# A planner's queue rule: of the operations that wait for a busy engine, the one that is due first goes first; attention is prepared five units ahead

## The chip, the cores and the metric

One core of a Trainium2 chip runs the kernel. The metric is the device time of one execution in microseconds (us), as the median of several. The engines that matter are PE (matrix products), DVE, ACT and POOL (elementwise work), and SP, which issues most DMAs. Each works through its own list of instructions in order; semaphores make an instruction wait for another engine.

## The reference

A decoder layer over 512 tokens of width 1024. After an RMS norm one projection gives the inputs of two attention mixers, eight heads of 64 each: one over blocks (here with its top-k taking every past block), one with three branches (compressed, selected, window). Gates and two more projections follow.

```python
h = rms_norm(x, norm_w[l]); proj = h @ w_in[l]
(q_a, k_a, v_a, z_a, q_b, kc, vc, ksl, vsl, kwn, vwn, gate_b, z_b, gate_m) = jnp.split(proj, split_points, axis=-1)
o_a = moba_mixer(rms_norm(heads(q_a), q_norm_a[l]), rms_norm(heads(k_a), k_norm_a[l]), heads(v_a), bias_a)
k_cmp = rms_norm(compress(heads(kc), cmp_pos_k[l], cmp_w1_k[l], cmp_w2_k[l]), k_norm_cmp[l])
v_cmp = compress(heads(vc), cmp_pos_v[l], cmp_w1_v[l], cmp_w2_v[l])
o_b = nsa_mixer(...)
y_a = o_a * jax.nn.silu(z_a); y_b = o_b * jax.nn.silu(z_b)
g_m = jax.nn.sigmoid(gate_m)
merged = g_m[..., :D_MODEL] * (y_a @ w_branch_a[l]) + g_m[..., D_MODEL:] * (y_b @ w_branch_b[l])
x = x + merged @ w_out[l]
```

All of it is float32. The kernel gets that accuracy from pairs of rounded numbers: a value is split into a high part (a rounded copy) and a low part (the value less that copy), and a product is three matmuls: high by high, low by high, high by low.

## The kernel before, in words

**Work.** Weights come from memory as 128x512 tiles (`wr`, six buffers). Each is split: a copy makes the high part `wh` (L350 on ACT or L354 on POOL), a subtraction the low part `wl` (L359, on DVE or POOL). The same two steps make `vh` and `vl` for the hidden layer of the compression (matmuls L839, L840). PE then runs the products (L384). Gate and output projections use a seven-product scheme for 2x2 block matrices, whose sums of weights are made in memory by DMAs that POOL and ACT issue (L572, L573).

**Attention** is 24 units: eight heads of the first mixer (units 0 to 7), then two groups of four heads with two branches each (units 8 to 15 and 16 to 23). A unit is, for four blocks of queries, scores (`sps`, L1001, L1002), bias and maximum (`sb`, L1020, DVE), exponential (`P`, L1035, ACT), reciprocal (L1038, DVE), scaling (L1039, POOL), and then transposes (`pt`, L1048), their split (`ph` L1060 on ACT, `pl` L1062 on DVE) and the products with the values (`O`, L1082). Before a unit can begin, its keys and queries are prepared: PE transposes them (`pq`, L924), ACT copies the high parts (`ks`, L955), DVE subtracts (`kx`, L957), ACT copies those to the other half of the partitions (`kx`, L960). The first unit of a group also needs the compressed scores (`scp`, L1180) and a softmax over them (`sc`, L1185 to L1204).

**Order.** Nothing is scheduled on the chip. While the program is written, a planner in it keeps a clock, `now`, and for ACT, DVE and POOL the time at which each comes free, from costs written in the code. PE's list is merged from several streams (attention, projections, compression): a stream whose next matmul has been ready for `MARGIN` ns is taken, by shares. All work of the other engines comes in chains (class `Chain`): steps that follow one another. A heap holds the chains by the time at which their next step can begin. `Chain.step` picks, of the engines that a step may run on, the one that would end it first, and books that engine at once, even if it is busy for some time yet. So steps are served in the order in which they became ready. Two kinds of chain are the exception: the splits of weights (`SLACK`, 3 us in all) and the prepared sums of the input (`XSLACK`, 4 us) step back while their engine is busy.

```python
end, k = min((ends(k, c.t, n), k) for k, n in cost.items())
wait = free[k.upper()] - 40 - c.t
if wait > 0 and c.slack > 0:
    c.slack -= wait
    c.t += wait
    c.push()
    return
```

The costs that the planner gives a 512-wide subtraction are 65 + 1.045 x 512 = 600 ns on DVE and 180 + 2.08 x 512 = 1245 ns on POOL (`either`). A rounded copy of a weight tile costs it 520 ns on ACT and 590 ns on POOL (L349 ff.).

While unit n runs, attention also drives the preparation of later units (`poll`, in `attention`): of the units n+1 up to n+`UNITS`-1 the first whose preparation is unfinished gets a step.

Of the kernel before, what the change touches and what calls it, by code (L numbers as in the profile page):

```python
# [38 lines left out]
SLACK = 3e3  # L39
XSLACK = 4e3  # L40
# [16 lines left out]
UNITS = 4  # L57
# [10 lines left out]
MARGIN = 600  # L68
# [36 lines left out]
def hybrid_kernel(ctx: ExitStack, tc: tile.TileContext, x, x0, xT, wtok, wchan, wz, wgate, gains, w1,  # L105
# [63 lines left out]
    class Chain:  # L169


        def __init__(c, t=None, held=False, slack=0.0):
            c.slack = slack
            c.t = now[0] if t is None else t
            c.q = deque()
            c.held = held
# [6 lines left out]
        def push(c):  # L183
            heapq.heappush(heap, (c.t, next(seq), c))
# [27 lines left out]
        def step(c):  # L212
# [10 lines left out]
            if cost is None:  # L223
                fn()
            else:
                if now[0] > 30e3:
                    cost = {k: n * SLOW[k.upper()] for k, n in cost.items()}
                end, k = min((ends(k, c.t, n), k) for k, n in cost.items())
                wait = free[k.upper()] - 40 - c.t
                if wait > 0 and c.slack > 0:  # L230
                    c.slack -= wait
                    c.t += wait
                    c.push()
                    return
                if k in lock:
                    lock[k] = end
                free[k.upper()] = end
                c.t = end + OUT[k.upper()] + LAT
                fn(ENG[k])
# [21 lines left out]
    def run_until(t):  # L261
        now[0] = max(now[0], t)
        while heap and heap[0][0] <= now[0]:
            heapq.heappop(heap)[2].step()
# [51 lines left out]
    class Stream:  # L316
# [19 lines left out]
        def split(w, upto):  # L336
            while len(w.chain) < min(upto, len(w.raws)):
# [8 lines left out]
                c = w.chain[i] = Chain(max(now[0], t), slack=SLACK if w is not W1_[0] and now[0] > 30e3 else 0.0)  # L346
# [367 lines left out]
    def proj_norm(name, gi, tags="gggg"):  # L714
        toks[name] = [None] * NT

        def emit(t, ps):
            toks[name][t] = att(name, F32)
            ch = Chain(now[0] + 230)
# [14 lines left out]
    def proj_v(name, outs, first=False):  # L734
# [3 lines left out]
        def emit(t, ps):  # L738
            ch = Chain(now[0] + 230)
# [56 lines left out]
    def compress_w(kv):  # L796
# [3 lines left out]
        def emit(ps):  # L800
            ch = Chain(now[0] + 230)
            for g in range(2):
                for l in range(2):
# [6 lines left out]
                    ch.do({"D": 335}, f, ps if g and l else None, None if g or l else "gmt")  # L810
            for i8 in range(2):
# [284 lines left out]
    def o_out(O, m, h):  # L1096
# [5 lines left out]
        ch = Chain(now[0] + 230)  # L1102
# [14 lines left out]
    def y_try(k):  # L1117
        if ("ys",) + k in done and ("zs",) + k in done:
            y, z = ys[k], zs[k]
            ch = Chain(max(done[("ys",) + k], done[("zs",) + k]))  # L1120
# [3 lines left out]
    def y_split(k):  # L1124

        def f():
            y, hi, lo = ys[k], att("yh"), att("yl")
            ch = Chain(max(now[0], done[("ym",) + k]))
# [221 lines left out]
    def x_prep(k):  # L1350
# [14 lines left out]
        c = Chain(held=True, slack=XSLACK)  # L1365
# [234 lines left out]
    def m_sums(k, fs):  # L1600
# [6 lines left out]
        c, d = x_sums(x1, x2, ta, tb)  # L1607
        for n_ in range(2):
            hi_lo(c, ta[:, h[n_]], ts[0][1][:, h[n_]], ts[0][2][:, h[n_]], n_)
# [193 lines left out]
```

## Time and profile before

| what | us |
|---|---|
| median of 3 runs (456.24 to 456.89) | 456.74 |
| the profiled execution's own time | 456.11 |
| its span, first to last instruction | 454.3 |
| first matmul with data begins | 4.50 |
| last matmul begins | 450.56 |
| PE clock granted | 1.00 throughout |

Times in the views are counted from the start of the span. The profiled execution has 1.8 us around its span and lies 0.63 us under the median. A matmul's end is modelled in the profile and matmuls overlap, so the distance from one matmul's start to the next tells more than its busy time: in an undisturbed stretch a 128x512 product begins every 0.23 us and a 128x256 product every 0.12 us, though they are shown as 0.40 and 0.28 us long.

### The profile page before, as it was taken

Reading aid. Unit: us, or ns where it says so; the run is one execution under the profiler, and the core shown is the slowest. Engines: PE = TensorE matmul, PEld = TensorE weight load, DVE = VectorE, ACT = ScalarE, POOL = GpSimd, SP = SyncE. Lnnn points to the kernel's source line nnn. Section 1 sums busy time; section 2 is a strip of 40 time slices with the busy share of each in tenths; the row PEclk is TensorE's granted clock in tenths of the full one; section 3 lists DMA queues with packets and bytes.
Section 4 is the critical chain, followed back from the end, with each engine's and each line's share of the span. In section 5 each row is a group of like instructions: output and inputs, shape, how many; then the busy total and the mean of one; then the engine's idle time right before and its main releaser. Section 6 shows DMA issues by size and latency. Waiting matters only on the chain.

```text
span 454.3 us, 8535 instructions
## 1 busy us (share of the span) xinstructions
PE 446.8 (98%) x2779; PEld 397.5 (87%) x2779; DVE 383.5 (84%) x938; ACT 301.8 (66%) x710; POOL 201.4 (44%) x239
## 2 busy tenths in 40 slices
PE   9999999999999999999999999999999999999996
PEld 7878888899778898888999999989988999998885
DVE  5998799889997787778899899978967599889783
ACT  6765768867978797376877677678755255454450
POOL 1264337865674572176775553754750212111000
PEclk9999999999999999999999999999999999999999
DMA  8876646787975869858968867975866888879862
GB/s 275 271 266 214 214 145 217 188 227 189 262 182 163 217 212 272 278 142 214 290 194 222 217 162 192 246 205 147 231 164 163 255 238 243 209 223 295 295 214 94
DMA packets 54221, 98.21 MB, mean 216 GB/s; under 512 B 5216, under 2 KB 8160, under 8 KB 54176
## 3 DMA queue, kind: packets, MB, share of 16 engines
q1 hardware_dynamic: 38944, 68.30, 46.3%
q0 software_dynamic: 7616, 14.68, 19.5%
q10 hardware_dynamic: 7616, 14.68, 9.4%
q8 instruction: 22, 0.36, 0.3%
q14 instruction: 23, 0.19, 0.1%
HBM read 90.69 MB, written 36.31 MB: 280 GB/s over the span
## 4 chain that ended last, share of the span: by engine, by line
PE 85%; DVE 8%; ACT 4%; issue 2%; POOL 0%; DVEq 0%; ACTq 0%; POOLq 0%
PE pgw L384 20%; PE pgt L384 14%; PE pbr L384 10%; PE po L384 8%; PE pgc L384 7%; PE O L1082 6%; PE pgf L652 5%; PE pt L1048 5%; PE sps L1001 3%; PE sps L1002 3%; DVE wl L359 1%; DVE vl L359 1%; ACT ks L955 1%; DVE sb L1020 1%; PE pq L924 1%
## 5 line engine op out<-in xcount | busy, mean ns | idle before, releaser
L359 DVE TENSOR_TENSOR wl<-wr,wh 128x512 fp32r<-128x512 f32 (+1 forms) x150 | 103.4, 704 | 4.5 <-ACT wh L350 4.0
L350 ACT CAST wh<-wr 128x512 fp32r<-128x512 f32 (+1 forms) x130 | 77.2, 609 | 15.8 <-PE po L384 4.7
L354 POOL TENSOR_SCALAR wh<-wr 128x512 fp32r<-128x512 f32 (+1 forms) x39 | 30.3, 787 | 80.5 <-DMA wr<-in_wtok 14.4
L1039 POOL TENSOR_SCALAR P<-P,sst,gate 128x512 f32<-128x512 f32 (+3 forms) x56 | 46.3, 828 | 40.2 <-DVE sst L1038 29.3
L1035 ACT ACTIVATE P<-sb,sst 128x512 f32<-128x512 f32 (+3 forms) x88 | 50.7, 577 | 17.3 <-DVE sst L1020 16.0
L1020 DVE CUSTOM_DVE_ANT_0 sb<-sps,T 128x512 f32<-128x512 f32 (+3 forms) x96 | 45.9, 482 | 14.8 <-PE sps L1002 13.6
L384 PE MATMUL pgt<-wl,hh 128*128 128x512 f32 (+2 forms) x160 | 56.3, 352 | 0.8 <-DVE wl L359 0.8
L384 PE MATMUL pgt<-wh,hh 128*128 128x512 f32 (+2 forms) x160 | 56.9, 356 | 0.0
L384 PE MATMUL pgt<-wh,hl 128*128 128x512 f32 (+2 forms) x160 | 56.2, 351 | 0.0
L384 PE MATMUL pgw<-th,wh 128*128 128x256 f32 x240 | 50.3, 285 | 0.0
L1060 ACT CAST ph<-pt 128x512 fp32r<-128x512 f32 (+2 forms) x72 | 33.8, 476 | 20.8 <-PE pt L1048 19.5
L384 PE MATMUL pgw<-hh,wh 128*128 128x256 f32 x160 | 45.8, 286 | 0.4 <-ACT c L1434 0.3
L384 PE MATMUL pgw<-hh,wl 128*128 128x256 f32 x160 | 45.0, 281 | 0.0
L384 PE MATMUL pgw<-hl,wh 128*128 128x256 f32 x160 | 44.8, 280 | 0.0
L1048 PE MATMUL pt<-cst,P 128*128 128x128 f32 x232 | 40.7, 273 | 0.3 <-DVE pl L1062 0.2
L384 PEld LDWEIGHTS pgw<-th,wh 128*128 128x128 f32 x240 | 40.0, 190 | 0.6 <-DVE gm L1493 0.2
L1062 DVE TENSOR_TENSOR pl<-pt,ph 128x512 fp32r<-128x512 f32 (+2 forms) x72 | 38.7, 548 | 1.9 <-ACT ph L1060 1.7
L427 POOL TENSOR_TENSOR nr<-nss,mhalf 128x8 f32<-128x8 f32 (+1 forms) x16 | 27.0, 1684 | 21.3 <-DVE nss L426 18.0
L384 PEld LDWEIGHTS pgt<-wl,hh 128*128 128x128 f32 x160 | 30.0, 188 | 5.6 <-DVE wl L359 1.2
L384 PE MATMUL pgw<-th,wl 128*128 128x256 f32 x120 | 33.9, 282 | 0.0
L384 PEld LDWEIGHTS pgt<-wh,hh 128*128 128x128 f32 x160 | 30.1, 188 | 3.8
L384 PEld LDWEIGHTS pgt<-wh,hl 128*128 128x128 f32 x160 | 30.1, 188 | 3.7
(268 smaller groups left out, 1290.7 us busy)
## 6 DMA issues: line engine op xcount, KB each, us to landing
wr<-wsum SPq DMA_DIRECT2D x56, 256.0 KB, 3.9
wr<-in_wtok SPq DMA_DIRECT2D x36, 256.0 KB, 4.9
wsum<-in_wgate ACTq DMA_DIRECT2D x16, 512.0 KB, 4.8
wsum<-wsum POOLq DMA_DIRECT2D x14, 512.0 KB, 7.7
wr<-in_wgate SPq DMA_DIRECT2D x24, 256.0 KB, 5.0
xsum<-th SPq DMA_DIRECT2D x16, 256.0 KB, 2.1
T<-rtab SPq DMA_DIRECT2D x16, 256.0 KB, 5.1
wr<-in_w SPq DMA_DIRECT2D x16, 256.0 KB, 4.5
```

The source lines that it names most:

```text
L350: e.copy(hi, raw)
L354: e.tensor_scalar(hi, raw, 1.0, 1.0, op0=ALU.mult, op1=ALU.mult)
L359: c.do({"D": cd(n)} if lead else either(n), lambda e, hi=hi, lo=lo, raw=raw: e.tensor_sub(lo, raw, hi.bitcast(F32))).mark((w, 1, i))
L384: nc.tensor.matmul(dst, sts[i][a], mvs[i][b], start=(start and i == a == b == 0), stop=(stop and i == n - 1 and b == 1), skip_group_check= ...
L427: c.do({"p": 430 + POWC * w}, lambda e: e.tensor_tensor(v(dst), v(ss), mhalf[:parts, :w], op=ALU.pow))
L1020: e.tensor_tensor_reduce(z["sb"][:, :L], sps[:, :L], T[:, S - L:], scale=-1.0, scalar=3e38, op0=ALU.add, op1=ALU.min, accum_out=st[:, 0, b ...
L1035: e.activation(pv(), z["sb"][:, :L], AF.Exp, bias=st[:, 0, b:b + 1], scale=-1.0, accum_out=st[:, 1, b:b + 1])
L1039: c.do({"P": 315 + 0.834 * L}, lambda e: e.tensor_scalar(pv(), pv(), st[:, 2, b:b + 1], g, op0=ALU.mult, op1=ALU.mult))
L1048: nc.tensor.transpose(pt[:, (b - kb) * P:(b - kb + 1) * P], u.p0 if u.p0 is not None and b == 0 else u.pb[:, POFF[b] + kb * P:POFF[b] + (k ...
L1060: e.copy(z["w"][0], pt[:, :w])
L1062: ch.do({"D": cd(w)}, lambda e: e.tensor_sub(z["w"][1], pt[:, :w], z["w"][0].bitcast(F32)), pt)
L1082: nc.tensor.matmul(O[0][:, S - n:], v.bitcast(F32) if kb == 3 else v, w, start=(u.first and kb == 0 and i == 0), stop=(u.last and kb == 3 ...
```

## The change

No operation is added or taken away, and no size changes. Four things differ, all in the planner.

Every chain may step back from a busy engine once the clock is past 30 us, however often; no allowance is used up. Chains that wait for the same engine come back at the same moment, 40 ns before it is free, and then the one with the earliest due time is served. A step is due when it first became ready, plus an allowance by kind (`LATE`): 6 us for splits of weights (3 us for those of the compression), 10 us for the sums of the input, 8 us for the windows of the compression, 1 or 2 us for norms, values, outputs and gates, and nothing for the steps of attention. `MARGIN` goes from 600 to 800 ns. `UNITS` goes from 4 to 6, so preparation may run up to five units ahead.

```diff
-SLACK = 3e3
-XSLACK = 4e3
+LATE = dict(w=6e3, w1=3e3, x=10e3, cmp=8e3, norm=1e3, v=1e3, out=1e3, y=2e3, gate=1e3, m=2e3)
...
-UNITS = 4
+UNITS = 6
...
-MARGIN = 600
+MARGIN = 800
...
-        def __init__(c, t=None, held=False, slack=0.0):
-            c.slack = slack
+        def __init__(c, t=None, held=False, late=0.0):
+            c.late, c.due = late, None
...
-            heapq.heappush(heap, (c.t, next(seq), c))
+            heapq.heappush(heap, (c.t, c.t if c.due is None else c.due, next(seq), c))
...
                 end, k = min((ends(k, c.t, n), k) for k, n in cost.items())
+                if c.due is None:
+                    c.due = c.t + c.late
                 wait = free[k.upper()] - 40 - c.t
-                if wait > 0 and c.slack > 0:
-                    c.slack -= wait
+                if wait > 0 and now[0] > 30e3:
                     c.t += wait
                     c.push()
                     return
+                c.due = None
...
-                c = w.chain[i] = Chain(max(now[0], t), slack=SLACK if w is not W1_[0] and now[0] > 30e3 else 0.0)
+                c = w.chain[i] = Chain(max(now[0], t), late=LATE['w'] if w is not W1_[0] else LATE['w1'])
...
-            ch = Chain(now[0] + 230)
+            ch = Chain(now[0] + 230, late=LATE["norm"])
...
-        c = Chain(held=True, slack=XSLACK)
+        c = Chain(held=True, late=LATE['x'])
```

The other lines of the diff give the chains of values, compression, outputs, gated outputs and merged sums their allowance in the same way.

What that does to the lists is seen in three places. The changed file's line numbers differ by one or two (L384 is L385 there, L960 is L962).

**ACT, ahead of the first scores of a new pair of heads.** `ks` is the last high copy of the transposed keys, `kx` the copy that the scores wait for; `wh` are weight copies, `ge`, `nraw` and `kb` belong to norms. Before:

```order
L955 CAST ks_1607<-pq_1585 64x512
L722 ACTIVATE ge_1675<-pgt_1614,nrx 128x24
L350 CAST wh_1565<-wr_1563 128x512
L695 ACTIVATE nraw_1700<-pgt_1614,rx 128x256
L350 CAST wh_1709<-wr_1600 128x512
L855 ACTIVATE gt_1708<-pu_1704 128x128
L697 ACTIVATE kb_1674<-nraw_1700 128x256
L350 CAST wh_1721<-wr_1649 128x512
L960 CAST kx_1606<-kx_1606 64x512
L960 CAST kx_1608<-kx_1608 64x512
```

The same place in the changed program:

```order
L957 CAST ks_1531<-pq_1500 64x512
L573 DMA wsum_149<-in_wgate 256x512
L698 ACTIVATE kb_1541<-nraw_1581 128x256
L684 CAST xs_1320<-XW_1318 128x4x64
L723 ACTIVATE ge_1609<-pgt_1543,nrx 128x24
L351 CAST wh_1596<-wr_1526 128x512
L696 ACTIVATE nraw_1631<-pgt_1543,rx 128x256
L698 ACTIVATE kb_1608<-nraw_1631 128x256
L962 CAST kx_1530<-kx_1530 64x512
L962 CAST kx_1532<-kx_1532 64x512
```

Two of the three weight copies that stood between `ks` and `kx` now stand elsewhere. Counted from the first `ks` of this pair, 17 rows stood ahead of `kx` before and 13 stand there now; four of the 17 were 128x512 copies of weights, and one of the 13 is.

**POOL, in the last head of the first mixer.** `P` is scaled block by block; `wl` and `vl` are subtractions of weights, `vh` copies. Before:

```order
L1039 TENSOR_SCALAR P_2244<-P_2244,sst_2253 128x512
L359 TENSOR_TENSOR wl_2330<-wr_1930,wh_2329 128x512
L1039 TENSOR_SCALAR P_2244<-P_2244,sst_2253 128x384
L354 TENSOR_SCALAR vh_2396<-wr_2334 128x512
L1039 TENSOR_SCALAR P_2244<-P_2244,sst_2253 128x256
L573 DMA wsum_149<-wsum_149 256x512
```

Now:

```order
L1041 TENSOR_SCALAR P_2213<-P_2213,sst_2221 128x512
L1041 TENSOR_SCALAR P_2213<-P_2213,sst_2221 128x384
L355 TENSOR_SCALAR vh_2313<-wr_2211 128x512
L1041 TENSOR_SCALAR P_2213<-P_2213,sst_2221 128x256
L355 TENSOR_SCALAR vh_2366<-wr_2296 128x512
L1041 TENSOR_SCALAR P_2213<-P_2213,sst_2221 128x128
```

The subtraction has left POOL and copies have come. Over the whole program POOL had 17 subtractions `wl` and 2 `vl` of 512 columns and has none; they are on DVE now. POOL's 512-wide copies go from 38 to 44 for `wh` and from 2 to 8 for `vh`, and ACT has as many fewer. Of the smaller steps DVE gains seven (`yl`, `pc`, `th`, `gm`, `qk`, `ch`, one sum of the input) and gives up nine (three `xs`, two `pcs`, one `kb`, three `pf`).

**PE, the compressed scores of the second group (unit 16).** `scp` are those scores, `pq` a transpose of queries, `pgw` the products of a gate projection. Before, in rows 1324 to 1330 of 2593:

```order
L924 MATMUL pq_3553<-cst,qb_2198 128x128
L1001 MATMUL sps_3563<-ks_2225,qs_2497 128x384
L1002 MATMUL sps_3563<-kx_2226,qs_2497 128x384
L1048 MATMUL pt_3566<-cst,P_3331 128x128 x3
L1180 MATMUL scp_3578<-kcs,qs_3437 128x64 x4
L384 MATMUL pgw_3458<-hh,wh_3376 128x256
L384 MATMUL pgw_3458<-hh,wl_3377 128x256
```

Now, in rows 1183 to 1189 of 2593:

```order
L1050 MATMUL pt_3253<-cst,P_2997 128x128
L1084 MATMUL O_3075<-ph_3158,vb_2378 128x384
L1084 MATMUL O_3075<-pl_3159,vb_2378 128x384
L1182 MATMUL scp_3264<-kcs,qs_3152 128x64 x4
L1084 MATMUL O_3075<-ph_3214,vb_2510 128x256
L1084 MATMUL O_3075<-pl_3215,vb_2510 128x256
L385 MATMUL pgw_3275<-hh,wh_3102 128x256
```

The four groups of `scp` stood in rows 1328 to 1446 and stand in rows 1186 to 1258: 142 to 188 rows earlier.

More of the change, by code (lines that the diff above doesn't have):

```diff
@@ L263, in run_until @@
         while heap and heap[0][0] <= now[0]:
-            heapq.heappop(heap)[2].step()
+            heapq.heappop(heap)[3].step()
     def alloc(tag, name, shape=(P, 512), dt=F32):
@@ L738, in emit @@
         def emit(t, ps):
-            ch = Chain(now[0] + 230)
+            ch = Chain(now[0] + 230, late=LATE["v"])
             for g in range(2 if name == "vb" else 0):
@@ L800, in emit @@
         def emit(ps):
-            ch = Chain(now[0] + 230)
+            ch = Chain(now[0] + 230, late=LATE["norm"])
             for g in range(2):
@@ L810, in emit @@
                     ch.do({"D": 335}, f, ps if g and l else None, None if g or l else "gmt")
+            ch.call(lambda: setattr(ch, "late", LATE["cmp"]))
             for i8 in range(2):
@@ L1101, in o_out @@
         y = ys[k]
-        ch = Chain(now[0] + 230)
+        ch = Chain(now[0] + 230, late=LATE["out"])
         z = {}
@@ L1119, in y_try @@
             y, z = ys[k], zs[k]
-            ch = Chain(max(done[("ys",) + k], done[("zs",) + k]))
+            ch = Chain(max(done[("ys",) + k], done[("zs",) + k]), late=LATE["y"])
             ch.do(either(512), lambda e: e.tensor_mul(y, y, z))
@@ L1127, in f @@
             y, hi, lo = ys[k], att("yh"), att("yl")
-            ch = Chain(max(now[0], done[("ym",) + k]))
+            ch = Chain(max(now[0], done[("ym",) + k]), late=LATE["y"])
             ch.do({"A": ca(512)}, lambda e: e.copy(hi, y))
@@ L1607, in m_sums @@
         c, d = x_sums(x1, x2, ta, tb)
+        c.late = d.late = LATE["m"]
         for n_ in range(2):
```

## The prediction

> **What bounds the kernel now.** I read the page's busy times first, then the busy times by stretch, then PE's rows in order of time wherever PE waits.
>
> ```profile
> PE 446.8 (98%) x2779; PEld 397.5 (87%) x2779; DVE 383.5 (84%) x938; ACT 301.8 (66%) x710; POOL 201.4 (44%) x239
> ```
>
> ```profile
> core 0: us, PE busy (x) PEld busy (x) DVE busy (x) ACT busy (x) POOL busy (x), PEclk, DMA share, GB/s
> 60.00:98.00 38.00, 38.00 (x202) 32.07 (x201) 34.91 (x92) 31.56 (x76) 28.34 (x32) 1.00 0.65 175
> 98.00:110.00 12.00, 12.00 (x96) 11.92 (x95) 10.82 (x25) 9.29 (x24) 7.70 (x11) 1.00 0.81 237
> 110.00:128.00 18.00, 15.92 (x95) 13.03 (x94) 17.77 (x48) 13.78 (x33) 9.24 (x9) 1.00 0.88 242
> 128.00:180.00 52.00, 51.70 (x340) 46.12 (x339) 42.26 (x116) 45.31 (x111) 30.83 (x34) 1.00 0.75 211
> 180.00:260.00 80.00, 80.00 (x559) 74.20 (x558) 70.13 (x199) 53.92 (x142) 45.30 (x53) 1.00 0.82 222
> 260.00:340.00 80.00, 79.65 (x562) 73.87 (x562) 68.25 (x200) 57.88 (x151) 47.16 (x57) 1.00 0.73 193
> ```
>
> PE sets the time: it is busy in 98% of the span, and its work isn't changed. So the change can only give or take PE's waits. One stretch stands out: from 110 to 128 us PE loses 18.00 - 15.92 = 2.08 us, and there DVE is busy in 17.77 of 18.00 us. Elsewhere DVE has room and PE hardly waits. The next rows are PE's own at its six longest gaps; columns are start, length, instruction.
>
> ```profile
> 121.58 0.39 PE L1001 MATMUL sps<-ks,qs 128*128 128x512 f32 x1
> 122.91 0.50 PE L1002 MATMUL sps<-kx,qs 128*128 128x512 f32 x1 [0.94 <-ACT kx L960]
> ...
> 125.72 0.39 PE L384 MATMUL pgt<-wh,hl 128*128 128x512 f32 x1
> 126.92 0.50 PE L384 MATMUL pgt<-wl,hh 128*128 128x512 f32 x1 [0.81 <-DVE wl L359]
> ...
> 175.60 0.28 PE L384 MATMUL pgt<-wl,hh 128*128 128x256 f32 x1
> 176.18 0.41 PE L850 MATMUL pu<-cst,hs 128*128 128x64 f32 x2 [0.30 <-DVE kx L957]
> ...
> 274.86 0.28 PE L384 MATMUL pgw<-th,wh 128*128 128x256 f32 x1
> 275.27 0.39 PE L384 MATMUL pgw<-hh,wh 128*128 128x256 f32 x1
> ...
> 318.36 0.28 PE L384 MATMUL pgw<-th,wh 128*128 128x256 f32 x1
> 318.83 0.41 PE L1048 MATMUL pt<-cst,P 128*128 128x128 f32 x2 [0.19 <-DVE pl L1062]
> ...
> 401.85 0.28 PE L384 MATMUL pgw<-th,wh 128*128 128x256 f32 x1
> 402.41 0.36 PE L384 MATMUL pgw<-hh,wh 128*128 128x256 f32 x1 [0.29 <-ACT c L1434]
> ```
>
> Start to start, less the 0.23 us (512 columns) or 0.12 us (256) that such a product takes undisturbed, the losses are 122.91 - 121.58 - 0.23 = 1.10, then 0.97, 0.46, 0.29, 0.35 and 0.44 us: 3.6 us together. With the smaller ones of the same kind I put all that order could win at **5 us**. What order can lose has no such end.
>
> **The change, part by part.** First the wait of 1.10 us for `kx`.
>
> ```profile
> 118.95 0.58 ACT L955 CAST ks<-pq 64x512 fp32r<-64x512 f32 x1
> ...
> 119.73 0.61 ACT L350 CAST wh<-wr 128x512 fp32r<-128x512 f32 x1
> ...
> 121.59 0.62 ACT L350 CAST wh<-wr 128x512 fp32r<-128x512 f32 x1
> 122.24 1.14 ACT L960 CAST kx<-kx 64x512 fp32r<-64x512 f32 x2
> ...
> 119.73 0.68 DVE L957 TENSOR_TENSOR kx<-pq,ks 64x512 fp32r<-64x512 f32 x1
> ```
>
> DVE's half of `kx` was done at 119.73 + 0.68 = 120.41, but ACT began its copy at 122.24: 1.83 us behind norms and weight copies that were ready earlier. In the order now, 13 rows instead of 17 stand between the first `ks` and `kx`, with one 128x512 weight copy instead of four: three copies of about 0.61 us, so 1.8 us, are gone from ahead of it, and a DMA issue and an `ot` copy of about half a microsecond each (an estimate from the `ks` row) have come in. That leaves about 0.8 us less on ACT. Between the same `pq` and these scores PE now has 54 products of 280 columns, where it had 27 of 280 and 18 of 512: 54 x 0.13 + 3 x 0.23 against 27 x 0.13 + 18 x 0.23 is about 7.7 against 7.7 us (0.13 by width, from 0.23 for 512), but eight more `hps` products of 0.12 us stand there too, about 1 us. So `kx` comes about 1.8 us better against PE, more than the 1.10 us it was late. I take **-1.0 us**; bounds 0, if DVE's half comes later by as much, and -1.1.
>
> Second the 0.97 us for `wl`. That subtraction was late twice over:
>
> ```profile
> 125.79 1.07 DVE L359 TENSOR_TENSOR wl<-wr,wh 128x512 fp32r<-128x512 f32 x1
> ...
> 125.58 0.73 POOL L706 TENSOR_TENSOR kb<-kb,gn 128x256 f32<-128x256 f32 x1
> ```
>
> It began only when 17.77 us of work in 18 had gone through DVE, and it took 1.07 us instead of its usual 0.7, while POOL ran a two-input operation. Giving weights six microseconds of grace does nothing for a late weight; only the work that no longer piles up before it helps. Between none and all of 0.97 I take half, **-0.5 us**.
>
> Third, the 0.29 us at 275. There the softmax of the second group's compressed scores runs through a DVE that is busy without a break:
>
> ```profile
> L1186 DVE TENSOR_TENSOR sc<-sc,scp x8: 278/282/288, 180.8 to 262.6; 128x128 f32<-128x128 f32 x8
> L1198 DVE TENSOR_REDUCE cd<-sc x2: 672/672/673, 187.7 to 270.5; 128x16 f32<-128x512 f32 x2
> L1204 DVE TENSOR_TENSOR pc<-sc,cd x1: 681/681/681, 277.4 to 277.4; 128x512 f32<-128x512 f32 x1
> ```
>
> The scores end at 262.6 and the last step comes at 277.4. The six-ahead rule moves the scores 142 to 188 PE rows forward, some 20 to 25 us at 0.12 to 0.14 us a row (an estimate from the stretch 260 to 340: 80 us for 562 products), into a stretch where DVE idles 80 - 70.13 = 9.9 us. The work is the same; this pile goes. I take **-0.3 us**, between 0 and -0.4; what it costs elsewhere is in the next term. On SP the bias load of that group's first head moves from row 165 to row 152 of the list, and weight loads queue behind it if its buffer is released late; I cost that at nothing, since none of PE's gaps above ends on a load.
>
> Fourth, the load on DVE.
>
> ```profile
> L359 DVE TENSOR_TENSOR wl<-wr,wh 128x512 fp32r<-128x512 f32 x145 | 101.0, 712 | 4.5 <-ACT wh L350 4.0
> L350 ACT CAST wh<-wr 128x512 fp32r<-128x512 f32 x123 | 74.3, 619 | 15.7 <-PE po L384 4.7 <-DMA wr<-in_wtok 3.3 <-DMA wr<-in_wgate 3.0
> L354 POOL TENSOR_SCALAR wh<-wr 128x512 fp32r<-128x512 f32 x38 | 29.7, 792 | 80.5 <-DMA wr<-in_wtok 14.4 <-DVE wl L359 14.1 <-DMA wr<-wsum 13.2
> L359 POOL TENSOR_TENSOR wl<-wr,wh 128x512 fp32r<-128x512 f32 x17 | 23.1, 1357 | 1.3 <-ACT wh L350 0.9
> ```
>
> The order moves 19 subtractions to DVE: 19 x 0.712 = **13.5 us** more there; the small steps that come and go (seven and nine) nearly cancel. POOL loses 19 x 1.357 = 25.8 and gains 12 x 0.792 = 9.5 us; ACT loses 12 x 0.619 = 7.4 us. Each lone subtraction gets faster, 0.71 for 1.36 us. Whether 13.5 us more on DVE cost anything depends on where they lie. POOL's own subtractions `wl`, by stretch:
>
> ```profile
> 110.00:128.00 18.00, 0.00 (x0) 1.00 0.88 242
> 180.00:260.00 80.00, 9.75 (x7) 1.00 0.82 222
> 260.00:340.00 80.00, 9.29 (x7) 1.00 0.73 193
> ```
>
>  In the stretches from 60 to 110 DVE idles 3.1 + 1.2 us, from 128 to 180 it idles 9.7, from 180 to 260 9.9, from 260 to 340 11.8: 35.7 us of cover against 13.5. Between 110 and 128 there is none, but POOL has no such subtraction there to give (x0). I take **+0.2 us**, between 0 and 2.6 (below).
>
> The Trainium skill weighs against this term: Perfetto Trace Analysis, section Optimizing Scalar/DVE Operations, says that with a saturated DVE it can pay to hand work to Scalar or even GPSIMD, and this change does the reverse; it adds that DVE and GPSIMD share a read port, so that the handing over may not help. The 1.07 us row above beside POOL's agrees with the second half. By the first half the term would be the rival's +2.6, by the second about 0.
>
> The other gaps (0.46, 0.35 and 0.44 us) and the first 4.5 us and the end I leave as they are. The larger margin for PE (0.8 us) I cost at nothing: PE has another stream to run meanwhile, which is where it loses nothing today; without that cover a wait of up to 0.2 us would be added each time.
>
> **Sum:** -1.0 - 0.5 - 0.3 + 0.2 = -1.6 us. The profiled execution took 456.11 us and would take 454.5; it lies 0.63 us below the median of the runs, 456.74, which would become 455.1. I forecast **455.1 us**, a gain of 0.35%. About 0.2%, or 0.9 us, is what a measurement of this kernel can tell from no change.
>
> **The rivals.** (1) *Slower: DVE becomes what PE waits for between 180 and 340.* POOL was the relief valve: a subtraction went there whenever DVE was booked up. Of the 17, 14 lie between 180 and 340, so about 14 x 0.712 = 10.0 us fall into the 160 us where DVE idles 21.7; it would be busy in 148.4 of 160, 93%. DVE at 10.82 of 12 (90%) cost PE nothing, at 17.77 of 18 (99%) it cost 2.08 us in 18. If the last 20 us of that kind come near 99%, PE loses 20/18 x 2.08 = 2.3 us there, and the 0.3 of the third term isn't won: +2.6. With half of the first two terms gone as well the median is 456.74 - 0.75 + 2.3 = 458.3. It decides from the point where PE idles over 2 us between 180 and 340. Against it: the order puts attention first, and each piece of work that PE needs soon waits for less. Chance 0.16. (2) *No change: the waits only move.* The 17.77 us of work in 18 are still to be done before the same products; an order can't shorten a full queue. `kx` comes early, and `wl` or a transposed block is late instead. 456.7 us, within 0.9 either way. For it: the chain of waits runs through DVE from 98 to 127 us. Against it: PE lost only 2.08 us there, and the pile held weights that weren't needed yet. Chance 0.24. (3) *More is won:* all gaps but the last (402) go, with the small ones: about 4.5 us, 452.2. Chance 0.12. (4) *Weights come late:* a split that may stand back 6 us holds one of six buffers, the next load starts late, and PE waits for `wl` as at 125.7, say four times 0.97: 460.6. Against it: the gate products need a tile only every 12 x 0.12 = 1.4 us, shared with attention until 340. Chance 0.04. That the change doesn't do what it says is excluded by the order: the lists of all engines differ.
>
> **How the numbers follow.** My forecast has 0.44. Faster by over 0.2%: 0.44 + 0.12 = 0.56; within: 0.24; slower: 0.20. The forecast's own bounds are the sums of the lower and upper ends, -2.5 and 0 (with +0.2): 454.2 to 456.9. To hold eight in ten I reach to 452.2 for the third rival and to 458.3 for the first, leaving out the fourth and the far ends.
>
> **What would show it.** Right: between 110 and 128 us PE's idle time falls below 1 us, the scores behind `kx` begin 0.23 us after those before them, and no wait for `wl` over 0.5 us stands there; the compressed scores of the second group end near 240 us instead of 262; DVE shows about 397 us, POOL about 185. Wrong: PE idles more than 1 us anywhere between 180 and 340 with `wl`, `pl` or `sb` as what ended the wait, or the loss between 110 and 135 is still 2 us, only in front of other products.

## The result, and the profile after

| | median, us | lowest to highest | against before on the same chip, 95% |
|---|---|---|---|
| before | 456.62 | 456.24 to 456.89 | |
| after | **460.45** | 459.65 to 460.90 | 1.0083 (1.0065 to 1.0100) |
| after, measured again on another chip | 459.49 | 458.10 to 460.50 | 1.0055 (1.0036 to 1.0074) |

The change makes the kernel slower, by 3.8 us in the first comparison and 2.5 in the second. The forecast was 455.1. Here and below, a single slow execution is left out of the median in three places: of after measured again (626.83 us at a clock of 0.66), and of two later runs (about 891 us each). The profiled execution of after took 460.9 us, with a span of 459.1.

First the page's busy times of after, then four of its stretches (columns as in the prediction: busy us and instructions of PE, PEld, DVE, ACT and POOL, then clock, DMA share, GB/s).

```profile
PE 448.5 (98%) x2779; PEld 399.4 (87%) x2779; DVE 394.0 (86%) x955; ACT 296.1 (65%) x698; POOL 194.0 (42%) x234
```

```profile
98.00:110.00 12.00, 11.64 (x93) 11.35 (x92) 11.55 (x31) 8.46 (x22) 6.93 (x11) 1.00 0.82 239
110.00:128.00 18.00, 16.35 (x109) 14.09 (x107) 16.74 (x45) 14.70 (x36) 12.59 (x15) 1.00 0.92 252
...
180.00:260.00 80.00, 76.97 (x506) 69.83 (x505) 70.79 (x203) 50.68 (x133) 37.60 (x46) 0.98 0.78 206
260.00:340.00 80.00, 79.51 (x586) 75.31 (x585) 72.52 (x198) 55.23 (x150) 44.06 (x53) 1.00 0.78 203
```

From 98 to 128 us PE idles 0.36 + 1.65 = 2.01 us, where it idled 2.08 before: nothing won. From 180 to 260, where it never idled, it now idles 3.03 us, and part of what it does there runs at a lower clock. PE's own rows at those places:

```profile
117.95 0.39 PE L1003 MATMUL sps<-ks,qs 128*128 128x512 f32 x1
118.18 0.39 PE L1004 MATMUL sps<-kx,qs 128*128 128x512 f32 x1
...
120.69 0.39 PE L385 MATMUL pgt<-wl,hh 128*128 128x512 f32 x1
121.69 0.38 PE L1003 MATMUL sps<-ks,qs 128*128 128x256 f32 x1 [0.61 <-DVE sst L1022]
...
122.49 0.40 PE L385 MATMUL pgt<-wl,hh 128*128 128x512 f32 x1
123.69 0.41 PE L1050 MATMUL pt<-cst,P 128*128 128x128 f32 x2 [0.80 <-DVE sst L1040]
...
228.00 0.28 PE L385 MATMUL pgw<-hl,wh 128*128 128x256 f32 x1
229.15 0.44 PE L1050 MATMUL pt<-cst,P 128*128 128x128 f32 x2 [0.87 <-POOL P L1041]
...
252.32 0.28 PE L385 MATMUL pgw<-th,wh 128*128 128x256 f32 x1
253.25 0.39 PE L385 MATMUL pgw<-hh,wh 128*128 128x256 f32 x1 [0.66 <-DVE gm L1486]
...
254.30 0.28 PE L385 MATMUL pgw<-hl,wh 128*128 128x256 f32 x1
256.07 1.12 PE L1050 MATMUL pt<-cst,P 128*128 128x128 f32 x4 [1.50 <-POOL P L1041]
```

The first product with the new `kx` follows the one with `ks` by 118.18 - 117.95 = 0.23 us: that wait is gone, as is the one for `wl`. In their place stand 121.69 - 120.69 - 0.23 = 0.77 us for a maximum and 0.97 us for a reciprocal on DVE. New are 229.15 - 228.00 - 0.12 = **1.03**, then **0.81** and **1.65** us, together 3.5. Two of the three end on POOL's scaling of `P`. A second profiled execution of after, at full clock, has the same three waits (1.03, 0.85 and 1.64 us) and took 458.10 us, so the waits alone don't make the whole of 460.9; the clock comes at the end of this document. POOL's rows there, and DVE's at the same time:

```profile
252.40 0.99 POOL L1041 TENSOR_SCALAR p<-p,sst,gate 128x128 f32<-128x128 f32 x1 [1.57 <-DVE sst L1040]
253.38 2.64 POOL L1041 TENSOR_SCALAR P<-P,sst,gate 128x128 f32<-128x128 f32 x1
```

```profile
253.13 0.80 DVE L1206 TENSOR_TENSOR pc<-sc,cd 128x512 f32<-128x512 f32 x1
253.85 0.41 DVE L1501 TENSOR_TENSOR gm<-pgw,R 128x256 f32<-128x256 f32 x1
254.19 0.67 DVE L1488 TENSOR_TENSOR gm<-gm,R 128x512 f32<-128x512 f32 x1
254.78 0.68 DVE L360 TENSOR_TENSOR wl<-wr,wh 128x512 fp32r<-128x512 f32 x1
255.39 0.15 DVE L1040 RECIPROCAL sst<-sst 128x1 f32<-128x1 f32 x1
255.46 0.40 DVE L1502 TENSOR_TENSOR gm<-gm,R 128x256 f32<-128x256 f32 x1
255.78 0.50 DVE L1212 TENSOR_TENSOR pcs<-pc,pcs 128x256 fp32r<-128x256 f32 x1
```

A scaling of 128x128 took 2.64 us, from 253.38 to 256.02, while DVE ran seven operations without a gap. Six of them read two inputs (one of these takes `pgw` from the memory in which PE leaves its products); the reciprocal reads one. How long such a scaling takes elsewhere is in the group of the eight that are called `p` (minimum, median and maximum in ns; before, then after):

```profile
L1039 POOL TENSOR_SCALAR p<-p,sst,gate x8: 445/447/870, 198.0 to 329.9; 128x128 f32<-128x128 f32 x8
```

```profile
L1041 POOL TENSOR_SCALAR p<-p,sst,gate x8: 447/660/2776, 192.9 to 330.3; 128x128 f32<-128x128 f32 x8
```

Half of these took 447 ns before, and none more than 870. Long scalings as such aren't new, though: of all 24 of 128x128, `p` and `P`, twelve took over 0.6 us before, up to 1.81, and eight in after. And a long one costs only where PE waits for it: the longest of after, 2.78 us at 330, made PE wait for nothing. New is that two of the long ones stand right in front of PE. I read this as DVE making POOL's scaling late, and that making PE late; the experiments below test it. Why DVE is so dense there is seen in the second group's softmax, which moved as forecast:

```profile
L1188 DVE TENSOR_TENSOR sc<-sc,scp x8: 274/279/282, 178.1 to 243.2; 128x128 f32<-128x128 f32 x8
...
L1206 DVE TENSOR_TENSOR pc<-sc,cd x2: 693/746/798, 185.3 to 253.1; 128x512 f32<-128x512 f32 x2
```

Its scores end at 243 instead of 262 us, its last step comes at 253 instead of 277. From 220 to 257 us (before, then after) DVE's idle time falls from 37 - 33.56 = 3.44 to 1.26 us, and PE's rises from nothing to 3.03:

```profile
220.00:257.00 37.00, 37.00 (x295) 36.10 (x294) 33.56 (x92) 27.89 (x75) 24.07 (x29) 1.00 0.82 212
```

```profile
220.00:257.00 37.00, 33.97 (x266) 32.60 (x265) 35.74 (x101) 24.23 (x63) 17.88 (x20) 0.98 0.77 206
```

### The profile page after: what moved, and what is told of

Same layout as the page of the kernel before. It is cut to its first block, busy times and chain, and to the rows that moved or that the text cites. A ratio compares the mean times of both kernels' runs of the same rounds, so it can differ in the third digit from the quotient of the medians.

```text
span 459.1 us, 8568 instructions
## 1 busy us (share of the span) xinstructions
PE 448.5 (98%) x2779; PEld 399.4 (87%) x2779; DVE 394.0 (86%) x955; ACT 296.1 (65%) x698; POOL 194.0 (42%) x234
## 4 chain that ended last, share of the span: by engine, by line
PE 76%; DVE 10%; ACT 6%; issue 3%; DMA 2%; POOL 2%; ACTq 0%; SPq 0%; DVEq 0%; POOLq 0%
PE pgw L385 16%; PE pgt L385 13%; PE pbr L385 8%; PE po L385 8%; PE pgc L385 7%; PE pgf L653 5%; PE pt L1050 5%; PE O L1084 5%; PE sps L1003 2%; PE sps L1004 2%; DVE wl L360 2%; DMA wr<-in_wgate 2%; DVE sb L1022 1%; ACT ks L957 1%; DVE pl L1064 1%
## 5 line engine op out<-in xcount | busy, mean ns | idle before, releaser
L360 DVE TENSOR_TENSOR wl<-wr,wh 128x512 fp32r<-128x512 f32 (+1 forms) x167 | 117.4, 718 | 1.6 <-ACT wh L351 1.5
L351 ACT CAST wh<-wr 128x512 fp32r<-128x512 f32 (+1 forms) x123 | 73.0, 609 | 18.8 <-DMA wr<-wsum 8.8
L1041 POOL TENSOR_SCALAR P<-P,sst,gate 128x512 f32<-128x512 f32 (+3 forms) x56 | 48.9, 875 | 58.9 <-DVE sst L1040 46.3
L355 POOL TENSOR_SCALAR wh<-wr 128x512 fp32r<-128x512 f32 (+1 forms) x46 | 35.3, 774 | 64.4 <-DVE wl L360 14.9
L385 PE MATMUL pgt<-wh,hh 128*128 128x512 f32 (+2 forms) x160 | 57.0, 356 | 0.1
L385 PE MATMUL pgt<-wl,hh 128*128 128x512 f32 (+2 forms) x160 | 56.2, 351 | 0.0
L385 PE MATMUL pgt<-wh,hl 128*128 128x512 f32 (+2 forms) x160 | 56.2, 351 | 0.0
L385 PE MATMUL pgw<-th,wh 128*128 128x256 f32 x240 | 49.3, 284 | 0.0
L385 PE MATMUL pgw<-hh,wh 128*128 128x256 f32 x160 | 46.3, 290 | 1.5 <-DVE gm L1486 0.7
L1050 PE MATMUL pt<-cst,P 128*128 128x128 f32 x232 | 41.9, 279 | 3.5 <-POOL P L1041 2.4
L385 PE MATMUL pgw<-hh,wl 128*128 128x256 f32 x160 | 45.0, 281 | 0.0
L385 PE MATMUL pgw<-hl,wh 128*128 128x256 f32 x160 | 44.8, 280 | 0.0
L385 PEld LDWEIGHTS pgw<-th,wh 128*128 128x128 f32 x240 | 39.7, 190 | 0.4
L1050 PEld LDWEIGHTS pt<-cst,P 128*128 128x128 f32 x232 | 29.7, 143 | 8.3 <-POOL P L1041 2.8
L385 PE MATMUL pgw<-th,wl 128*128 128x256 f32 x120 | 33.9, 282 | 0.0
L385 PEld LDWEIGHTS pgt<-wl,hh 128*128 128x128 f32 x160 | 30.0, 188 | 4.3
L385 PEld LDWEIGHTS pgt<-wh,hh 128*128 128x128 f32 x160 | 30.1, 188 | 3.8 <-ACT nraw L696 0.3
```

What stands on the lines that cost most here:

```text
L351: e.copy(hi, raw)
L355: e.tensor_scalar(hi, raw, 1.0, 1.0, op0=ALU.mult, op1=ALU.mult)
L360: c.do({"D": cd(n)} if lead else either(n), lambda e, hi=hi, lo=lo, raw=raw: e.tensor_sub(lo, raw, hi.bitcast(F32))).mark((w, 1, i))
L385: nc.tensor.matmul(dst, sts[i][a], mvs[i][b], start=(start and i == a == b == 0), stop=(stop and i == n - 1 and b == 1), skip_group_check= ...
L1041: c.do({"P": 315 + 0.834 * L}, lambda e: e.tensor_scalar(pv(), pv(), st[:, 2, b:b + 1], g, op0=ALU.mult, op1=ALU.mult))
L1050: nc.tensor.transpose(pt[:, (b - kb) * P:(b - kb + 1) * P], u.p0 if u.p0 is not None and b == 0 else u.pb[:, POFF[b] + kb * P:POFF[b] + (k ...
```

## The experiments

Four questions: which part of the change costs the time, whether it is the engine of the 19 moved subtractions, whether it is their second input, and whether the place counts. Ratios are to before on the same chip, with 95% intervals. Four runs (four units, six units alone, the subtractions on DVE, and the scalings on DVE) were weighed between a port theory (two-input operations on DVE hold up POOL's scaling) and a pile theory (six units ahead heap work on DVE in front of units that are running).

### Which part of the change

Four units again, rule and margin kept:

```diff
-UNITS = 6
+UNITS = 4
```

> The changed kernel (460.5 us) with preparation three units ahead again (UNITS 4), the rest of the change kept. Pile theory (preparing the second group earlier piles its softmax onto 246 to 256 us, where PE lost about 4 us): the loss there goes, 456 to 457 us. Port theory (the subtractions that went from POOL to DVE hold up POOL's scaling of P, wherever preparation stands): the time stays near 460, 459 to 461 us, with waits of PE for P elsewhere.

Six units in the kernel before, nothing else:

```diff
-UNITS = 4
+UNITS = 6
```

> The kernel before (456.6 us) with UNITS 6 alone. Pile theory: 459 to 460 us, PE loses 3 us or more in the stretch where the second group's softmax now runs. Port theory: within 1 us of 456.6, since POOL keeps its 17 subtractions.

The rule alone, and after with the old margin:

```diff
-UNITS = 6
+UNITS = 4
...
-MARGIN = 800
+MARGIN = 600
```

> Kernel after with attention prepared four units ahead again and the margin of 600: the due-time rule is the only thing left of the change. Its planner puts 2 of the weight subtractions on POOL where before put 22. Load theory (the rule sends some 20 subtractions more to DVE, and the two-input subtractions there hold DVE and POOL's scaling up): about as slow as the same rule with four units and the margin of 800 (457.7 measured), so 457.3 to 458.6, with waits for POOL's scaled P or DVE's scores left in the attention. Margin theory (the margin of 800 cost part of it): 456.2 to 457.0. If the rule itself gains what the prediction said, with no cost of the load: 455.0 to 455.6.

```diff
-MARGIN = 800
+MARGIN = 600
```

> Kernel after with the margin of 600 that before had; rule and six units stay, and 2 subtractions are planned on POOL. If the margin is nothing, as the prediction had it: 460 to 461. If it costs what it costs beside four units (457.69 against 457.33): 459.5 to 460.4. If margin and units together make the wait at 254: 457.5 to 459.

| | median, us | ratio |
|---|---|---|
| rule alone | 457.33 | 1.0022 (1.0006 to 1.0039) |
| rule and margin | 457.69 | 1.0037 (1.0026 to 1.0049) |
| six units alone | 457.06 | 1.0029 (1.0013 to 1.0045) |
| rule and six units | 459.14 | 1.0057 (1.0042 to 1.0072) |
| all three: after | 460.45 and 459.49 | 1.0083 and 1.0055 |

The rule and the six units each cost some 0.2 to 0.3%, and together about their sum. What the margin costs is not told from nothing. Neither theory holds for both: 457.69 us with four units lies between the two ranges, and 457.06 with six units alone is what the port theory had. Each combination waits at other places. With six units alone, for one, the longest wait is in front of a block's scores, 240.39 - 238.98 - 0.12 = 1.29 us, and none of the three above appears at that size.

### Which engine has the subtractions

The moved subtractions were my next suspect. In before, all 22 of POOL's are issued on DVE, in the same order:

```diff
-... lambda e, hi=hi, lo=lo, raw=raw: e.tensor_sub(lo, raw, hi.bitcast(F32)))
+... lambda e, hi=hi, lo=lo, raw=raw: nc.vector.tensor_sub(lo, raw, hi.bitcast(F32)))
```

> The kernel before with its order kept, except that the 22 subtractions of weights which it runs on POOL are issued on DVE at the same place. Port theory: POOL's scaling gets slower (mean of L1039 up by 3% or more) and PE waits for P or behind DVE: 457.5 to 460 us. Pile theory: nothing is prepared earlier, 456 to 457.5 us.

461.65 us, 1.0120 (1.0098 to 1.0143), more than either theory had. That seemed to settle it: 5.5 us lost by the engine alone. The other direction followed: in after, and in the rule alone, the 19 go back to POOL.

```diff
+BACK = {(16, 1), (16, 4)} | {(170, i) for i in (47, 50, 53, 54, 56, 63, 66, 68, 73, 74, 81, 90, 92, 95, 97, 103, 105)}
...
-... e.tensor_sub(lo, raw, hi.bitcast(F32)))
+... (nc.gpsimd if b else e).tensor_sub(lo, raw, hi.bitcast(F32)))
```

> Kernel after in its own order of emission; only, the 19 weight subtractions that before had on POOL and after on DVE are issued on POOL again at their places. Nothing else is moved. Load theory: DVE is rid of 13.5 us of work, the waits for gm near 252 and for P near 254 and 228 shrink or go, and the time falls from 460.4 to 456.5 to 458.0. Order theory (the order of the rule and the early pile of six units cost the time, whatever engine has the subtractions): 459.5 to 461, with the waits at their places; POOL, with 19 subtractions that its plan did not know of, may even give more.

> The rule alone (four units, margin of 600) with the same 19 subtractions issued on POOL. Load theory: the rule's gain without its price, 455.2 to 456.6, at or below the kernel before. Order theory: no better than the rule alone without this edit, 457 to 459.

464.41 us, 1.0171 (1.0148 to 1.0194), and 459.78, 1.0085 (1.0057 to 1.0113): both slower than without the edit, so the load theory failed as I had put it. A subtraction at a place where POOL's plan has no room stands ahead of a scaling, and PE waits 234.23 - 232.42 - 0.12 = 1.69 us (POOL's row in the first of the two, ahead of the scaling, then PE's rows):

```profile
232.48 1.27 POOL L361 TENSOR_TENSOR wl<-wr,wh 128x512 fp32r<-128x512 f32 x1
```

```profile
232.42 0.28 PE L386 MATMUL pgw<-hl,wh 128*128 128x256 f32 x1
234.23 0.44 PE L1051 MATMUL pt<-cst,P 128*128 128x128 f32 x2 [1.53 <-POOL P L1042]
```

That could be the missing plan's fault, so three more let the planner know: a higher price on POOL in before (8 there instead of 22), a lower one in after (23 instead of 3) and in the rule alone (20 instead of 2).

```diff
-c.do({"D": cd(n)} if lead else either(n), ...
+c.do({"D": cd(n)} if lead else ({"d": cd(n), "P": 2 * cg(n)} if len(w.raws) == 170 and i >= 52 else either(n)), ...
```

> Kernel before with its own rule, four units and margin 600, but its planner is told that a subtraction of the weights costs twice as much on POOL from piece 52 on, so that it plans 8 of them there instead of 22; 14 go to DVE, and everything else is planned around that. Placement theory (each subtraction more on DVE costs, by its time and its second input, though the plan knows of it): 457.2 to 459.5, with new waits for scaled P or scores between 180 and 340. Order theory (the due-time rule and the early pile cost the time, where the subtractions run is nothing): 456.0 to 456.9.

```diff
-c.do({"D": cd(n)} if lead else either(n), ...
+c.do({"D": cd(n)} if lead else {"d": cd(n), "P": 0.9 * cg(n)}, ...
```

> Kernel after (rule, six units, margin 800); its planner reckons a subtraction of the weights on POOL at nine tenths of the cost, so that it plans 23 of them there instead of 3, and everything else around that. Placement theory: about what six units alone cost with 22 subtractions on POOL (457.06 measured), so 456.5 to 458.2. Order theory: 459.5 to 461, as after.

> The rule alone (four units, margin 600), with the same nine tenths: 20 subtractions of the weights are planned on POOL instead of 2. Placement theory: the rule without its price, 455.4 to 456.6, no slower than before. Order theory: 457 to 458.5, as the rule alone (457.33 measured).

463.44 us, 1.0140 (1.0112 to 1.0167); 468.48, 1.0263 (1.0228 to 1.0298); 465.92, 1.0205 (1.0186 to 1.0225). All three are slower than either theory had them, the last two by 7 us or more. A planned move, either way, costs more than the whole change. Every new plan waits at new places; in the last it is DVE that is held up, a subtraction of 0.68 us for 2.71, while POOL runs one operation behind another (DVE's row, POOL's, PE's):

```profile
133.75 2.71 DVE L360 TENSOR_TENSOR vl<-wr,vh 128x512 fp32r<-128x512 f32 x1
```

```profile
133.80 0.94 POOL L817 TENSOR_TENSOR XW<-X,cst 128x248 f32<-128x248 f32 x1
134.50 1.41 POOL L355 TENSOR_SCALAR wh<-wr 128x512 fp32r<-128x512 f32 x2
```

```profile
133.29 0.40 PE L385 MATMUL pgt<-wh,hl 128*128 128x512 f32 x1
137.11 0.80 PE L385 MATMUL pgt<-wl,hh 128*128 128x512 f32 x1 [3.43 <-DVE wl L360]
```

In the first it is no collision at all. Its longest wait, 323.55 - 320.96 - 0.12 = 2.47 us, is for a `gm` of DVE, and POOL stood idle until 0.27 us before its end (PE's rows, then POOL's next operation after 5.25 idle us):

```profile
320.96 0.28 PE L384 MATMUL pgw<-th,wh 128*128 128x256 f32 x1
323.55 0.39 PE L384 MATMUL pgw<-hh,wh 128*128 128x256 f32 x1 [2.32 <-DVE gm L1461]
```

```profile
323.28 0.45 POOL L1039 TENSOR_SCALAR p<-p,sst,gate 128x128 f32<-128x128 f32 x1 [5.25 <-DVE sst L1038]
```

So the count of subtractions on an engine explains no sign, and the collision of DVE and POOL doesn't explain all of these runs: a wait can also come from the order alone. What made these three so slow is not taken apart.

### The second input

In after, the 19 moved subtractions stay on DVE at their places, but become reductions that read one input; their low halves are then not the residuals:

```diff
-... e.tensor_sub(lo, raw, hi.bitcast(F32)))
+... e.tensor_reduce(lo, raw.rearrange("p (n o) -> p n o", o=1), op=ALU.max, axis=mybir.AxisListType.X) if b else e.tensor_sub(lo, raw, hi.bitcast(F32)))
```

> Kernel after in its own order; the 19 moved subtractions stay on DVE but read one input instead of two: a reduction over an axis of length one takes the place of the subtraction (so the low halves of 19 weight tiles are not the residuals that the reference needs), with about the same time on DVE, if the 128x512 reduction to 128x8 of 682 ns is a guide. It tells DVE's time from the second input. Second-input theory (two-input subtractions on DVE stretch POOL's scaling): most of the excess goes, 457 to 458.5, and scalings of P beside these 19 run at their short times. Load theory (DVE's time is what counts): 459.5 to 461, as after.

458.00 us, 1.0041 (1.0027 to 1.0055): 2.4 us under after's first median, though the interval overlaps that of after measured again. Of the three waits, 1.03 becomes 0.46 and 0.81 becomes 0.38; the third stays at 1.65. None of the 19 runs beside that scaling; the two-input operations that do are others, which the new order puts there. The other way to free POOL's scaling of a collision is to take it off POOL. In after, the scalings of 128x128 are issued on DVE:

```diff
-c.do({"P": 315 + 0.834 * L}, lambda e: e.tensor_scalar(pv(), pv(), st[:, 2, b:b + 1], g, op0=ALU.mult,
+c.do({"P": 315 + 0.834 * L}, lambda e: (e if b else nc.vector).tensor_scalar(pv(), pv(), st[:, 2, b:b + 1], g, op0=ALU.mult,
```

> The changed kernel with its order kept word for word, except that the scaling of the 128x128 block of P (24 of them) is issued on DVE at the same place of the program instead of POOL. Port theory: PE's two waits for P (1.0 us at 228, 1.7 at 254) and the half clock after the second (1.3 us) go: 457 to 458.5 us. Pile theory: DVE, the engine with the pile, gets 24 short operations more (about 0.2 us each, an estimate from the reciprocal's 0.15), so PE waits as before or longer: 460 to 462 us.

460.38 us, 1.0105 (1.0078 to 1.0133): nothing won, as the pile theory had it. The waits for POOL are gone, but the scalings now stand in DVE's full list, and PE waits for DVE instead: 1.08 us for `gm` near 254, which was 0.81, and 230.47 - 229.47 - 0.12 = 0.88 us for a scaled `P`:

```profile
229.47 0.28 PE L385 MATMUL pgw<-hl,wh 128*128 128x256 f32 x1
230.47 0.66 PE L1050 MATMUL pt<-cst,P 128*128 128x128 f32 x4 [0.72 <-DVE P L1041]
```

### The place

What was open now: DVE's time from 220 to 257 us, the second input there, or the order as such. Nine subtractions of that stretch become one-input reductions in one run, and copies on ACT in the other; all else is after.

```diff
+ONE = (60, 61, 62, 63, 66, 68, 69, 70, 71)
...
-... e.tensor_sub(lo, raw, hi.bitcast(F32)))
+... e.tensor_reduce(lo, raw.rearrange("p (n o) -> p n o", o=1), op=ALU.max, axis=mybir.AxisListType.X) if b else e.tensor_sub(lo, raw, hi.bitcast(F32)))
```

> Kernel after, its order untouched. Nine subtractions of weights that run on DVE between 225 and 256 us, where DVE has no idle time, stay at their places on DVE but become reductions with one input (so these nine low halves aren't the residuals that the reference needs). DVE's own work there stays about the same (0.66 instead of 0.68 us each); only POOL's scalings are less held up. If the second input of DVE's operations makes the waits for P at 228 and 254: both shrink to under 0.5 us, 457.5 to 459. If DVE is simply full there, whatever its operations read: the waits stay, 459.5 to 461.

```diff
-... e.tensor_sub(lo, raw, hi.bitcast(F32)))
+... nc.scalar.copy(lo, raw) if b else e.tensor_sub(lo, raw, hi.bitcast(F32)))
```

> The same nine, as copies on ACT (again not the residuals): DVE is rid of about 6 us of work between 225 and 256, and of their second inputs. If a full DVE there makes the loss: the waits at 228, 252 and 254 go, with the low clock behind the last, 456 to 457.5; by so much more than the one-input run gains is DVE's time, the rest its second input. If the loss is made elsewhere, by the due-time order as such: 459 to 461.

Controls: nine others in after (pieces 49 to 57), as copies on ACT and as reductions; six of the nine in before, on ACT; and after itself once more. In all these runs but the last, the low halves concerned are not the residuals.

```diff
-ONE = (60, 61, 62, 63, 66, 68, 69, 70, 71)
+ONE = tuple(range(49, 58))
```

> A control of the place: nine other subtractions of weights (pieces 49 to 57, between 160 and 215 us, where DVE has idle time) as copies on ACT, in the order of after. If the place counts, as DVE is full only between 220 and 257: 459.8 to 461, as after. If DVE's sum over the whole kernel counts: as much gained as with the nine between 225 and 256.

> Kernel after with nine one-input reductions in place of subtractions (not the residuals), like the run with nine between 225 and 256 us, but at pieces 49 to 57, between 160 and 215 us, where DVE has idle time. If the second input counts only where DVE is full and PE waits for POOL: as after on the same chip, within 0.5 us, the waits at 228, 252 and 254 unchanged. If it counts wherever it is: as fast as with the nine between 225 and 256, some 3 us faster than after.

```diff
+ONE = (60, 61, 62, 69, 70, 71)
```

> A control in the kernel before: those six of the nine that before has on DVE too, as copies on ACT, in the order of before. If the relief in after is of a wait that the change made: within 0.5 us of before (456.0 to 456.9). If any 4 us off DVE near 240 make any order faster: 453.5 to 455.5.

> Kernel after, unchanged, for more times and a second profile on the chip of the next run: 459.5 to 461. If the low clock behind the wait at 254 is part of what the change costs, it shows again and the clock is 0.995 to 0.997 in most executions; if it comes and goes, executions with a clock of 0.999 or more are some 1.3 to 1.7 us faster than those with it.

| | median, us | ratio |
|---|---|---|
| after, nine at 225 to 256 with one input | 457.26 | 1.0015 (1.0005 to 1.0024) |
| after, the same nine on ACT | 457.92 | 1.0028 (1.0014 to 1.0042) |
| after, nine elsewhere on ACT | 458.89 | 1.0055 (1.0036 to 1.0074) |
| after, nine elsewhere with one input | 459.21 | 1.0047 (1.0029 to 1.0064) |
| after again | 459.49 | 1.0055 (1.0036 to 1.0074) |
| before, six of the nine on ACT | 457.66 | 1.0028 (1.0013 to 1.0042) |

The nine at that place, with one input, win 2 to 3 us of what the change had lost; nine elsewhere, with one input or on ACT, can't be told from after measured again, and their profiles keep all three waits (1.2, 0.84 and 1.65 us with one input, 1.1, 0.84 and 1.65 on ACT). In the run with one input at the place, the three are 0.30, 0.37 and 0.94 us; I had expected the last under 0.5. DVE has no more idle time in the run with one input than in after (36.45 of 37 us busy), and yet PE waits less. The stretch, POOL's scaling before the wait near 254, and DVE's rows beside it:

```profile
220.00:257.00 37.00, 35.86 (x281) 34.22 (x280) 36.45 (x104) 25.99 (x68) 16.38 (x21) 1.00 0.80 214
```

```profile
253.03 1.94 POOL L1042 TENSOR_SCALAR P<-P,sst,gate 128x128 f32<-128x128 f32 x1
```

```profile
253.84 0.67 DVE L1489 TENSOR_TENSOR gm<-gm,R 128x512 f32<-128x512 f32 x1
254.44 0.67 DVE L361 TENSOR_REDUCE wl<-wr 128x512 fp32r<-128x512 f32 x1
```

The scaling ended at 253.03 + 1.94 = 254.97, some 0.53 us after the reduction with one input began; alone it takes 0.45. The run on ACT takes both the time and the second inputs of the nine off DVE, which now has 6 us to spare. Two of the three waits are gone there. But the scaling near 254 takes as long as in after, since the operations beside it are others and still stand in a row. It ends at 252.67 + 2.65 = 255.32, in DVE's gap of 1.27 us, and PE waits 1.26 us for it:

```profile
220.00:257.00 37.00, 35.20 (x278) 33.74 (x276) 31.02 (x95) 29.74 (x76) 17.19 (x21) 1.00 0.79 218
```

```profile
252.67 2.65 POOL L1042 TENSOR_SCALAR P<-P,sst,gate 128x128 f32<-128x128 f32 x1
```

```profile
253.75 0.68 DVE L1489 TENSOR_TENSOR gm<-gm,R 128x512 f32<-128x512 f32 x1
254.35 0.15 DVE L1041 RECIPROCAL sst<-sst 128x1 f32<-128x1 f32 x1
254.42 0.40 DVE L1503 TENSOR_TENSOR gm<-gm,R 128x256 f32<-128x256 f32 x1
254.74 0.41 DVE L1213 TENSOR_TENSOR pcs<-pc,pcs 128x256 fp32r<-128x256 f32 x1
256.43 0.56 DVE L1023 CUSTOM_DVE_ANT_0 sb<-sps,T 128x384 f32<-128x384 f32 x1 [1.27 <-PE sps L1005]
```

So with DVE as full as in after, taking away nine second inputs at this place is enough to win most of the loss back, and a free DVE doesn't shorten a scaling that has two-input operations beside it. Whether DVE's time counts as well is not settled: the interval of the run on ACT overlaps that of the run with one input and those of the controls, and its copies bring a new wait of 0.86 us for ACT.

In before, six such copies win nothing; they cost 1.1 us (1.0028), which neither expectation had, with a new wait of 0.64 us for ACT. So taking work off DVE near 240 didn't make that order faster. The run with one input has no such counterpart in before.

No version beat before. Of those that change order or engines alone, the nearest is the rule alone, at 1.0022.

## Why the prediction was wrong, by its own steps

**First and second term, -1.0 and -0.5.** The mechanism was right: `kx` and `wl` are in time. The gain was zero, as the second rival had it. From 98 to 128 PE idles 2.01 us instead of 2.08, mostly for a maximum and a reciprocal on DVE; from 110 to 128 it is 1.65, where I had said below 1. What I didn't ask is what is late next on an engine that had been busy 17.77 of 18 us.

**Third term, -0.3.** The 0.29 us at 275 are gone, and the second group's softmax came 19 to 24 us earlier, as said. I booked this pile as gone; it was moved into 230 to 256 us, in front of units that were running.

**Fourth term, +0.2: this step failed.** It set 13.5 us of subtractions against 35.7 us of DVE's idle time, summed from 60 to 340 us. The cover has to stand where the work falls. From 220 to 257 before had 3.44 us of idle time, and there both the pile and part of the subtractions came down. PE lost 3.5 us at 228, 252 and 254, in place of 0.2, and beyond the upper bound of 2.6. That bound, moreover, was left out of the range: with it the sum reaches 456.74 + 2.6 = 459.3, still under the measured time. The bound also missed a second price. I had the row of a subtraction on DVE stretched to 1.07 us beside POOL's work, and took it as an argument for fewer on POOL. That the same collision runs the other way, and holds up a scaling that PE waits for, was in the profile of before as well: in the stretch where the softmax stood then, one of these scalings took 1.47 us instead of 0.45, with PE busy elsewhere. The load of the subtractions isn't the whole of it either: with the 19 at one input the wait at 254 stayed, so that one belongs to the pile, whose cost elsewhere I had put into this term.

```profile
276.89 1.47 POOL L1039 TENSOR_SCALAR P<-P,sst,gate 128x128 f32<-128x128 f32 x1
```

The first rival (DVE as what PE waits for between 180 and 340, decided where PE idles over 2 us there) named the place and the sign; PE idles 3.03 + 0.49 us. Its price, 2.3 us, was too small; it was taken from a stretch in which about half of the 2.08 us was a wait for `kx` on ACT. Part of its mechanism was wrong: DVE is busy 143.3 of the 160 us, not 148.4, PE waits mostly for POOL, held up by DVE, and with DVE just as full about a quarter of the loss is left. The waits that I named as the sign of being wrong, for `wl`, `pl` or `sb`, are not the ones that came.

The Trainium skill bears on this: SBUF — State Buffer, section Who interferes with whom, says that a DVE instruction with two SBUF inputs contends with a GpSimd instruction that reads SBUF, and one with at most one input doesn't. The run with nine one-input reductions agrees, 457.26 against 460.45 and 459.49 us. The Trainium skill, SBUF — State Buffer, section Summary: rules for kernel authors, says that the second of the two to issue is blocked until the first finishes. Here the scaling lasted through several DVE instructions in a row, 2.64 us.

**The margin, at nothing.** 459.14 us with 600 against 460.45 and 459.49 with 800: not told from nothing, as predicted.

**The numbers.** DVE's busy time came out as 394.0 (397 forecast), POOL's as 194.0 (185): two thirds of the excess are its scalings, which took 6.2 us longer in sum.

What stays open: why the rule alone costs 0.2%, and what the last 0.15% are once the collision at 228 to 256 is relieved. Both are spread over waits below 1.3 us at several places, and no run took them apart. Open is also how much of the first median's 3.8 us is the clock.

## What to carry to other kernels

Cover for moved work counts only at the place where it lands: compare idle time stretch by stretch, where two moved pieces of work can meet, never as a sum over the kernel. When operations move to DVE, look at what POOL does at that moment and who waits for it; a short POOL operation can stand through a whole row of two-input DVE operations. And in a kernel whose order fits its engines to within a few tenths of a microsecond, ask of every removed wait which one is next.

## What the runs showed of the hardware that I had not expected

**A row of operations on one engine can hold up an operation of the other for much longer than one of them lasts.** A 128x128 scaling on POOL took 2.64 us beside two-input DVE operations (0.45 alone), and in another order a DVE subtraction took 2.71 us beside three POOL operations in a row (0.68 alone). The subtraction ended at 136.46, some 0.55 us after the last of the three (135.91), so it seems to have got no turn between them; the scaling ended while DVE's row still ran.

**PE's clock fell behind two short waits, but not each time.** In the first profile of after the clock from 255 to 260 us was 0.66 on average, behind waits of 0.81 and 1.65 us; in the second, with a scaling of 2.64 us and a wait of 1.64, it was full (the stretch of the first, then of the second):

```profile
255.00:260.00 5.00, 3.93 (x20) 3.83 (x21) 3.42 (x11) 2.56 (x6) 3.25 (x4) 0.66 0.62 110
```

```profile
254.00:259.00 5.00, 3.66 (x30) 3.58 (x31) 4.16 (x13) 2.91 (x8) 3.53 (x4) 1.00 0.57 112
```

Of the executions of after on the second chip, those with a mean clock of 0.998 or more took 458.10, 458.56 and 459.49 us, those with 0.995 or 0.996 took 460.09 and 460.50: about 1.6 us more. On the first chip the difference was smaller: 459.65 and 460.45 at 0.999, 460.46 and 460.90 at 0.996. So a wait may cost more than its length, now and then; what brings the clock down was not tested. The Trainium skill, TensorE: Matmul & The Clock Gate, section Why this matters for your kernels, has the clock fall after pauses of some 3 us; here it fell behind two waits of 0.81 and 1.65 us within 4 us, in one of two profiled executions.
